# Two products of v in one accumulator bank, and three element-wise steps and one inverse step held behind read-outs, in a hybrid attention/recurrence block

## The chip, the cores and the metric

The kernel runs on one core of a Trainium2 chip, in one launch. The metric is the device time of that core in microseconds (us), the median of several runs. TensorE (PE in the profile) multiplies matrices into accumulator banks, VectorE (DVE), ScalarE (ACT) and GpSimd (POOL) do the element-wise work, and SyncE (SP) issues most DMAs. [...]

## The reference, cut to what matters

One block over 1024 tokens of width 1024: a modulated norm, an input projection, an attention with 8 heads beside a recurrence with 8 heads, a gated merge, and a feed-forward part. The change lies in the attention's v columns and in the recurrence:

```
proj = u @ w_in                       # q, k, v, f | r, k, v, xw, xa, xg | gates
q, k, v, f = split(p_fox)             # v: 1024 x 512, 8 heads of 64
...
kk = k * k_k;  kk = kk / norm(kk)     # recurrence, per head
k_mod = k * (1 + (a - 1) * k_a)
b_vec = kk * a;  a_vec = -kk
def step(state, inp):
    sa = state @ a_t
    state = state * w_t + outer(sa, b_t) + outer(v_t, k_t)
    return state, state @ r_t
```

## The kernel before

All large products are made in a split form: an operand is kept as a high part `hi` and a remainder `lo`, both in TensorE's reduced fp32 type, and a product is `hi*hi + hi*lo + lo*hi`.

The recurrence is done in chunks of 64 tokens. Its eight units are pairs `(p, hf)`: four pairs of heads and two halves of the sequence. A name such as `E2_1` or `kr3_0` carries p and hf at its end. `pre` prepares a unit: decays by a scan (`cum`, `el`, `en`), the scaled keys `bk`, `ar`, products within a chunk (`E`), and the inverse of a unit triangular matrix, 31 steps of two DVE instructions on `E32` and `t32` with the matrix in `M32`, which goes through DRAM and back (`sm`, `M32`, then `se`, `TT`). `main` then runs the chain of states: `xi`, `zi`, `uw`, `mz`, and the eight steps `sp`, after which the output is normalised (`mu`, `va`).

TensorE's instruction order is written out: the class `Weave` keeps a planned clock and puts background products between the recurrence's small ones, one matmul at a time. The background is, in order, the projections for r, k, v of the next units (`ps_rkv`), q and k of the attention (`qk_steps`), then v of the attention (`v_steps`), then the gates (`gate_steps`). The order on DVE, ACT, POOL and SP in this part is chosen by a scheduler when the kernel is built; `add_manual_dep` with `NOSYNC` tells it that one instruction must stand behind another on the same engine, and costs no semaphore.

`v_steps(w, j)` makes half j of v (256 columns) for eight groups t of 128 tokens. A product is 24 matmuls of 128x256, in the first half of an accumulator tile `ps` from `big`, which has two banks that take turns. Its read-out is an ACT copy of the high part into `vs` and a DVE subtraction of the remainder, then a DMA to `d_v`. Product t of half j is called `v{j}_{t}`, its read-out `vs{j}_{t}`.

`shifted` and `qk_steps` are the other users of `big`; their last DVE step reads a bank out (`k`, `r`, `v` of a unit in the one, `ql` in the other). The steps in `pre` that the change touches are these:

```
ts(al, al, V("k_a", p), oka[:, p : p + 1], op0=ALU.mult, op1=ALU.add)
tt(al, al, kk, op=ALU.mult)
tt(bk[:, :, 1, :], c3(al), c3(en), op=ALU.mult)
...
nc.vector.tensor_copy(QA[:, :, 0, :], c3(q))
```

Of the kernel before, what the change touches and what calls it, by code (L numbers as in the profile page):

```python
# [12 lines left out]
ALU = mybir.AluOpType  # L13
# [5 lines left out]
NH = 512  # L19
# [115 lines left out]
def hybrid_block(ctx: ExitStack, tc: tile.TileContext, a, out):  # L135
    nc = tc.nc
    weave = Weave()
    ctx.enter_context(tc.manual_schedule(engines={mybir.EngineType.PE}))

    def mm(o, lhsT, rhs, start, stop, more=False):  # L140

        weave.mm_cost(o, lhsT, rhs)
        nc.tensor.matmul(o, lhsT, rhs, start=start, stop=stop, skip_group_check=more)  # L143
# [5 lines left out]
    def f32(ap):  # L149
        return ap.bitcast(F32)  # L150
# [17 lines left out]
    def V(name, i=0, n=1):  # L168
        o, _ = VEC[name]
        return vec[:, o + i : o + i + n]  # L170
# [78 lines left out]

    marks = {}  # L250
    held = []

    def behind(i, x):
        if x in marks:
# [91 lines left out]
    u = (u_hi, u_lo)  # L346
# [27 lines left out]
    with ExitStack() as es:  # L374
# [4 lines left out]
        def big(name):  # L379
            return pb.tile([128, NH], F32, tag="big", name=name)  # L380
# [4 lines left out]
        def shifted(w, ti, hf, dst, prev, name, by_kt=False):  # L385

            ps = big(f"ps_{name}{hf}")
            yield from gemm_steps(ps, w, u, slice(hf * NH, hf * NH + NH), by_kt=by_kt)
            sh = shp.tile([128, NH + 1], F32, tag="sh", name=f"sh_{name}{hf}")
            if hf == 0:  # L390
                nc.vector.memset(sh[:, 0:1], 0.0)
            else:
                nc.vector.tensor_copy(sh[:, 0:1], prev)
            nc.scalar.activation(sh[:, 1 : NH + 1], ps, AF.Copy, scale=V("mu", ti))
            if hf == 0:
                nc.gpsimd.tensor_copy(prev, sh[:, NH : NH + 1])
            marks["bank"] = stt(dst, ps, omu[:, ti : ti + 1], sh[:, 0:NH], op0=ALU.mult, op1=ALU.add)

        rkv, got, last_col = {}, {}, {}

# [13 lines left out]
        def qk_steps(w, i):  # L414
            sc_ = 0.125 if i < 4 else 1.0
            for hf in range(2):
                cs = slice(hf * NH, hf * NH + NH)
                ps = big(f"qk{i}_{hf}")
                yield from gemm_steps(ps, w, u, cs)
                hi = gsp.tile([128, NH], F32R, tag="sp0", name=f"qh{i}_{hf}")  # L420
                nc.scalar.activation(hi, ps, AF.Copy, scale=sc_)
                lo = gsp.tile([128, NH], F32R, tag="sp0", name=f"ql{i}_{hf}")
                stt(lo, ps, sc_, f32(hi), op0=ALU.mult, op1=ALU.subtract)
                h0 = 2 * (i % 4)
                for t, k, r0 in ((hi, 0, 0), (lo, 0, 64), (hi, 2, 0)) if i < 4 else ((hi, 1, 0), (hi, 1, 64), (lo, 3, 0)):
                    for h in range(2):
                        nc.sync.dma_start(f32(d_st[h0 + h, k, r0 : r0 + 64, cs]), f32(t[h * 64 : h * 64 + 64, :]))
# [274 lines left out]
        def c3(ap):  # L702
            return ap.rearrange("p (c s) -> p c s", s=CH)
# [23 lines left out]
        def pre(k, p, hf):  # L727
# [41 lines left out]
            tt(bk[:, :, 0, :], c3(kr), c3(en), op=ALU.mult)  # L769
            nc.gpsimd.tensor_copy(bk[64:128, :, 2, :], bk[64:128, :, 0, :])  # L770
            tt(ar[:, 1], c3(rr), el[:, :, 1:], op=ALU.mult)
            ts(al, al, V("k_a", p), oka[:, p : p + 1], op0=ALU.mult, op1=ALU.add)
            tt(al, al, kk, op=ALU.mult)
            tt(bk[:, :, 1, :], c3(al), c3(en), op=ALU.mult)
            pcd = chunk_tile("pcd", 3, NCU)
            nc.gpsimd.tensor_copy(pcd, el[:, :, CH])
            rkb = tmp("ksq")
# [33 lines left out]
            for s in range(31):  # L811
                J, W = s // 4 + 1, 31 - s
                tv = t32[:, 0 : J * W].rearrange("p (j w) -> p j w", w=W)
                tt(tv, E32[:, 0:J, s : s + 1].to_broadcast([128, J, W]),  # L814
                   M32[:, s : s + 1, s + 1 : 32].to_broadcast([128, J, W]), op=ALU.mult)
                tt(E32[:, 0:J, s + 1 : 32], E32[:, 0:J, s + 1 : 32], tv, op=ALU.add)  # L816
            se = scr.tile([2, NCU, 2, 32, 32], F32, tag="se", name=f"se{n}")
            for g in range(4):
# [31 lines left out]
            for c in range(NCU):  # L850
                for h in range(2):
                    mm(q[HS[h], c * CH : c * CH + CH], E[HS[1 - h], c, h, 0, :], UV[HS[1 - h], c, h, :], start=True, stop=True)
            nc.vector.tensor_copy(QA[:, :, 0, :], c3(q))
            bp = gen(f"bs{n}")
            yield from head_sums(bp, rkb, tmp("kr", dt=F32R), tmp("al", dt=F32R), True)
            bon = tmp("bon", bufs=2)
# [113 lines left out]
        def v_steps(w, j):  # L970

            for t in range(8):
                ts_ = slice(t * 128, t * 128 + 128)
                ps = big(f"v{j}_{t}")
                n = 0
                for wi, xi in ((0, 0), (0, 1), (1, 0)):
                    for kt in range(KT):
                        c0 = (kt % 4) * 256
                        mm(ps[:, 0:256], u[xi][:, kt, ts_], w[kt // 4][wi][:, c0 : c0 + 256], start=n == 0, stop=n == 23)
                        n += 1  # L980
                        yield
                vs = gsp.tile([128, 4, 2, 64], F32R, tag="sp0", name=f"vs{j}_{t}")
                pv = ps[:, 0:256].rearrange("p (h d) -> p h d", d=64)
                nc.scalar.copy(vs[:, :, 0, :], pv)
                tt(vs[:, :, 1, :], pv, f32(vs[:, :, 0, :]), op=ALU.subtract)
                nc.sync.dma_start(f32(d_v[4 * j : 4 * j + 4, :, t, :]).rearrange("h p x -> p h x"), f32(vs).rearrange("p h a d -> p h (a d)"))
# [730 lines left out]
    ps = wo_do(3, 3)  # L1717
# [380 lines left out]
```

## Time and profile before

| | |
|---|---|
| median of 3 runs | 1640.1 us (1639.86 to 1641.15) |
| profiled execution, its own time | 1639.56 us |
| its span | 1637.8 us |
| mean granted TensorE clock | 0.996 |
| PE busy | 1600.6 us, 98% |
| DVE busy | 1214.5 us, 74% |
| ACT busy | 827.8 us, 51% |
| POOL busy | 157.4 us, 10% |

The v products lie between 319 and 447 us from the span's start; the recurrence with its background ends near 613 us, the attention near 815 us, and the rest is the merge and the feed-forward part. In rows of the timeline the first number is the start in us, the second the length of the row; "x8" means eight instructions of one kind that follow each other; a bracket at the end gives the idle time of the engine before the row and what ended it.

### The profile page before, as it was taken

To read this page: it belongs to the slowest core of one execution; us is meant where nothing else is said; L and a number is where in the kernel's file an instruction comes from. 1 tells how busy PE (TensorE), PEld (TensorE's weight loads), DVE (VectorE), ACT (ScalarE), POOL (GpSimd) and SP (SyncE) were. 2 spreads that over 40 slices of the span, in tenths; PEclk is the share of its full clock that TensorE was granted. 3 is DMA by queue.
4 is the path that set the end of the run, shared out by engine and by line. 5 is a ranking of instruction groups with operands and counts; after the bars stand their busy time and mean duration, and the time that the engine had idled before them with its cause. 6 is when DMAs were issued, how large, how long until landed. Compare 5 with 4: busy or idle time off the path is not lost.

```text
span 1637.8 us, 25963 instructions
## 1 busy us (share of the span) xinstructions
PE 1600.6 (98%) x9678; PEld 1334.4 (81%) x9678; DVE 1214.5 (74%) x2343; ACT 827.8 (51%) x1557; POOL 157.4 (10%) x189
## 2 busy tenths in 40 slices
PE   8999999999999999999999999999999999999998
PEld 7777787888978788888878888888888888888886
DVE  5786787878876536888679548987777777886677
ACT  5563344444455656778623225644444444555455
POOL 0011101111111011333122000000000000000000
PEclk9999999999999999999999999999999999999999
DMA  9496645543333336434197521232332332675363
GB/s 341 128 328 204 177 130 143 141 114 92 115 104 96 97 121 165 128 103 121 44 357 264 187 81 39 71 135 97 114 105 97 101 105 96 232 249 161 122 212 109
DMA packets 123542, 238.79 MB, mean 146 GB/s; under 512 B 42188, under 2 KB 51284, under 8 KB 123416
## 3 DMA queue, kind: packets, MB, share of 16 engines
q1 hardware_dynamic: 114936, 218.77, 41.2%
q0 software_dynamic: 8480, 18.37, 4.2%
q8 instruction: 76, 1.25, 0.3%
q14 instruction: 50, 0.41, 0.1%
HBM read 172.57 MB, written 64.50 MB: 145 GB/s over the span
## 4 chain that ended last, share of the span: by engine, by line
PE 71%; DVE 6%; ACT 2%; issue 1%; DMA 1%; SPq 1%; POOL 0%; DVEq 0%; POOLq 0%; ACTq 0%
PE X L143 15%; PE D L143 13%; PE Y L143 7%; PE gt L143 6%; PE wo L143 5%; PE br L143 4%; PE rk_ps L143 4%; PE W L143 4%; PE ps_rkv L143 3%; PE ov L143 2%; PE lg L143 2%; PE tp L147 1%; PE v L143 1%; PE sp L143 1%; DVE quads L1082 1%
## 5 line engine op out<-in xcount | busy, mean ns | idle before, releaser
L143 PE MATMUL D<-op,op 128*128 128x512 f32 x924 | 209.8, 389 | 0.0
L143 PEld LDWEIGHTS D<-op,op 128*128 128x128 f32 x924 | 173.3, 188 | 36.3 <-DVE op L1302 0.3
L143 PE MATMUL X<-T_m,S 128*128 128x512 f32 x440 | 107.1, 390 | 0.0
L143 PEld LDWEIGHTS X<-T_m,S 128*128 128x128 f32 x440 | 82.4, 188 | 17.8 <-ACT T_m L1781 0.5
L1301 ACT CAST op<-g 128x512 fp32r<-128x512 f32 x77 | 47.8, 621 | 73.0 <-PE D L143 48.2
L1302 DVE TENSOR_TENSOR op<-g,op 128x512 fp32r<-128x512 f32 x77 | 53.0, 689 | 40.8 <-ACT op L1301 40.8
L1560 DVE SCALAR_TENSOR_TENSOR c<-ab,vec,c 128x512 f32<-128x512 f32 x88 | 65.8, 750 | 18.4 <-ACT c L1563 16.8
L814 DVE TENSOR_TENSOR t<-E,M 128x60 f32<-128x60 f32 (+24 forms) x248 | 56.4, 227 | 27.5 <-DMA M<-sm 21.5
L1526 DVE TENSOR_TENSOR A<-ur,A 128x512 fp32r<-128x512 f32 x64 | 44.0, 689 | 38.3 <-ACT A L1522 38.2
L1526 DVE TENSOR_TENSOR S<-ur,S 128x512 fp32r<-128x512 f32 x66 | 45.5, 691 | 35.2 <-ACT S L1522 35.1
L1522 ACT CAST S<-ur 128x512 fp32r<-128x512 f32 x66 | 41.0, 622 | 57.3 <-DVE ur L1515 30.3
L298 DVE TENSOR_TENSOR lo_in<-raw_in,hi_in 128x512 fp32r<-128x512 f32 x84 | 57.6, 726 | 15.8 <-PE gt L143 4.8
L143 PE MATMUL Y<-T_h,A 128*128 128x512 f32 x264 | 63.4, 389 | 0.0
L143 PE MATMUL Y<-T_h,S 128*128 128x512 f32 x264 | 63.3, 389 | 0.0
L1122 DVE TENSOR_TENSOR tl<-tp,th 128x512 fp32r<-128x512 f32 (+1 forms) x80 | 50.0, 631 | 15.3 <-ACT th L1119 14.9
L1522 ACT CAST A<-ur 128x512 fp32r<-128x512 f32 x64 | 39.6, 621 | 42.9 <-PE X L143 33.4
L296 ACT CAST hi_in<-raw_in 128x1024 fp32r<-128x1024 f32 x42 | 43.8, 1048 | 34.2 <-PE qk L143 14.0
L816 DVE TENSOR_TENSOR E<-E,t 128x60 f32<-128x60 f32 (+24 forms) x248 | 56.0, 226 | 6.3
L143 PE MATMUL W<-B_f,A 128*128 128x512 f32 x252 | 60.6, 389 | 0.0
L143 PE MATMUL X<-B_b,A 128*128 128x512 f32 x252 | 60.5, 389 | 0.0
L143 PEld LDWEIGHTS Y<-T_h,S 128*128 128x128 f32 x264 | 49.6, 188 | 10.3
L143 PEld LDWEIGHTS Y<-T_h,A 128*128 128x128 f32 x264 | 49.5, 188 | 10.3
(491 smaller groups left out, 4143.1 us busy)
## 6 DMA issues: line engine op xcount, KB each, us to landing
raw_in<-in_w_in SPq DMA_DIRECT2D x50, 512.0 KB
wm<-in_w_mod SPq DMA_DIRECT2D x48, 512.0 KB
ur<-in_w_up SPq DMA_DIRECT2D x44, 512.0 KB
g<-d_g SPq DMA_DIRECT2D x35, 512.0 KB
d_g<-gs SPq DMA_DIRECT2D x44, 256.0 KB
d_g<-c SPq DMA_DIRECT2D x33, 256.0 KB
d_st<-qh SPq DMA_DIRECT2D x64, 128.0 KB
stA<-d_st POOLq DMA_DIRECT2D x8, 1024.0 KB, 7.3
```

The lines of the kernel that those rows point to most:

```text
L143: nc.tensor.matmul(o, lhsT, rhs, start=start, stop=stop, skip_group_check=more)
L147: nc.tensor.transpose(o, i, eye)
L296: nc.scalar.copy(hi, raw)
L298: nc.vector.tensor_tensor(lo[:, c : c + NH], raw[:, c : c + NH], f32(hi[:, c : c + NH]), op=ALU.subtract)
L814: tt(tv, E32[:, 0:J, s : s + 1].to_broadcast([128, J, W]), M32[:, s : s + 1, s + 1 : 32].to_broadcast([128, J, W]), op=ALU.mult)
L816: tt(E32[:, 0:J, s + 1 : 32], E32[:, 0:J, s + 1 : 32], tv, op=ALU.add)
L1122: tt(tl[:, 0:w], tp[:, 0:w], f32(th[:, 0:w]), op=ALU.subtract)
L1301: nc.scalar.copy(hi, src)
L1302: tt(lo, src, f32(hi), op=ALU.subtract)
L1522: nc.scalar.copy(hi, src)
L1526: tt(lo, src, f32(hi), op=ALU.subtract)
L1560: stt(c, ab[:, x + hf * NH : x + hf * NH + NH], V("conv_w", 22 * x + i), c, op0=ALU.mult, op1=ALU.add)
```

## The change

Three edits, none of which adds or removes a step of the computation. First, two consecutive products of `v_steps` share one accumulator tile: product t with t even takes the first 256 columns, t + 1 the second. Second, in `pre` the three DVE steps on `al` and `bk` are kept in a list for 3000 units of the planned clock; the next DVE read-out in `shifted` or `qk_steps` is given to the scheduler as something that they must stand behind. Third, the first of the 31 inverse steps of a unit must stand behind DVE's copy of `q` into `QA`.

```diff
+    soft = []
+
+    def evac_done(i):
+        for x, t in soft:
+            if weave.now - t < 3000:
+                tc.add_manual_dep(x.ins, i.ins.name, NOSYNC)
+        soft.clear()
+        return i
+    first_step = []
+
+    def after_this(i):
+        for x in first_step:
+            tc.add_manual_dep(x.ins, i.ins.name, NOSYNC)
...
-            marks["bank"] = stt(dst, ps, omu[:, ti : ti + 1], sh[:, 0:NH], op0=ALU.mult, op1=ALU.add)
+            marks["bank"] = evac_done(stt(dst, ps, omu[:, ti : ti + 1], sh[:, 0:NH], op0=ALU.mult, op1=ALU.add))
...
-                stt(lo, ps, sc_, f32(hi), op0=ALU.mult, op1=ALU.subtract)
+                evac_done(stt(lo, ps, sc_, f32(hi), op0=ALU.mult, op1=ALU.subtract))
...
-            ts(al, al, V("k_a", p), oka[:, p : p + 1], op0=ALU.mult, op1=ALU.add)
-            tt(al, al, kk, op=ALU.mult)
-            tt(bk[:, :, 1, :], c3(al), c3(en), op=ALU.mult)
+            soft.clear()
+            soft.append((ts(al, al, V("k_a", p), oka[:, p : p + 1], op0=ALU.mult, op1=ALU.add), weave.now))
+            soft.append((tt(al, al, kk, op=ALU.mult), weave.now))
+            soft.append((tt(bk[:, :, 1, :], c3(al), c3(en), op=ALU.mult), weave.now))
...
-                tt(tv, E32[:, 0:J, s : s + 1].to_broadcast([128, J, W]),
-                   M32[:, s : s + 1, s + 1 : 32].to_broadcast([128, J, W]), op=ALU.mult)
+                i = tt(tv, E32[:, 0:J, s : s + 1].to_broadcast([128, J, W]),
+                       M32[:, s : s + 1, s + 1 : 32].to_broadcast([128, J, W]), op=ALU.mult)
+                if k == 0 and s == 0:
+                    first_step.append(i)
...
-            nc.vector.tensor_copy(QA[:, :, 0, :], c3(q))
+            after_this(nc.vector.tensor_copy(QA[:, :, 0, :], c3(q)))
+            first_step.clear()
...
-                ps = big(f"v{j}_{t}")
+                if t % 2 == 0:
+                    pair = big(f"v{j}_{t}")
+                ps = pair[:, t % 2 * 256 : t % 2 * 256 + 256]
...
-                        mm(ps[:, 0:256], u[xi][:, kt, ts_], w[kt // 4][wi][:, c0 : c0 + 256], start=n == 0, stop=n == 23)
+                        mm(ps, u[xi][:, kt, ts_], w[kt // 4][wi][:, c0 : c0 + 256], start=n == 0, stop=n == 23)
...
-                pv = ps[:, 0:256].rearrange("p (h d) -> p h d", d=64)
+                pv = ps.rearrange("p (h d) -> p h d", d=64)
```

TensorE's order stays the same instruction for instruction; what changes there is the tile that a v product writes and what it waits for. On PE, at the products `v0_4` and `v0_5` of the first half, this stands before (a bracket names the engines on whose semaphores the instruction waits; `sp1_0` is the chain of states of unit 1_0):

```order
L143 MATMUL v0_4_3684<-hi_v00_3289,u_hi_107 128x256 [waits DVE_49]
L143 MATMUL v0_4_3684<-hi_v00_3289,u_hi_107 128x256 x3
L143 MATMUL v0_4_3684<-hi_v01_3296,u_hi_107 128x256 x4
L143 MATMUL v0_4_3684<-hi_v00_3289,u_lo_108 128x256 x4
L143 MATMUL v0_4_3684<-hi_v01_3296,u_lo_108 128x256 x4
L143 MATMUL v0_4_3684<-lo_v00_3290,u_hi_107 128x256 x3
L143 MATMUL sp1_0_3605<-S1_00_3693,Mt_1241 128x64 [waits DVE_49,Activation_49]
L143 MATMUL v0_4_3684<-lo_v00_3290,u_hi_107 128x256
L143 MATMUL v0_4_3684<-lo_v01_3297,u_hi_107 128x256 x4
L143 MATMUL v0_5_3718<-hi_v00_3289,u_hi_107 128x256 [waits DVE_49]
L143 MATMUL v0_5_3718<-hi_v00_3289,u_hi_107 128x256 x3
```

The same place on PE now, where the tile of `v0_5` carries the name of `v0_4`:

```order
L143 MATMUL v0_4_3682<-hi_v00_3289,u_hi_107 128x256 [waits PE_49]
L143 MATMUL v0_4_3682<-hi_v00_3289,u_hi_107 128x256 x3
L143 MATMUL v0_4_3682<-hi_v01_3296,u_hi_107 128x256 x4
L143 MATMUL v0_4_3682<-hi_v00_3289,u_lo_108 128x256 x4
L143 MATMUL v0_4_3682<-hi_v01_3296,u_lo_108 128x256 x4
L143 MATMUL v0_4_3682<-lo_v00_3290,u_hi_107 128x256 x3
L143 MATMUL sp1_0_3604<-S1_00_3691,Mt_1241 128x64 [waits DVE_49,Activation_49]
L143 MATMUL v0_4_3682<-lo_v00_3290,u_hi_107 128x256
L143 MATMUL v0_4_3682<-lo_v01_3297,u_hi_107 128x256 x4
L143 MATMUL v0_4_3682<-hi_v00_3289,u_hi_107 128x256 [waits DVE_49]
L143 MATMUL v0_4_3682<-hi_v00_3289,u_hi_107 128x256 x3
```

Nothing moved, but the waits did. Counted through the semaphores, `v0_5` waited before for DVE's remainder step of `vs0_3`, the product that had its bank earlier; now it waits for that of `vs0_4`, the product just ahead of it. `v0_4` waited before for `vs0_2`; now it waits for nothing on DVE. The other pairs are alike.

On DVE, where unit 0_0 is in its inverse and the remainder `ql5_1` of a q/k product is read out (`bon0_0` is a bonus term, `cum0_1` the scan of the next unit, `lo_in17` a weight's remainder), this stands before:

```order
L814 TENSOR_TENSOR t320_0_1513<-E320_0_1511,M320_0_1506 128x50
L816 TENSOR_TENSOR E320_0_1511<-E320_0_1511,t320_0_1513 128x2x25
L814 TENSOR_TENSOR t320_0_1513<-E320_0_1511,M320_0_1506 128x48
L857 TENSOR_TENSOR bon0_0_1688<-bs0_0_1665,v00_636 128x512
L744 SCALAR_TENSOR_TENSOR cum0_1_1694<-cst2_117,cum0_1_1694 128x256 x2
L816 TENSOR_TENSOR E320_0_1511<-E320_0_1511,t320_0_1513 128x2x24
L298 TENSOR_TENSOR lo_in17_1725<-raw_in17_1722,hi_in17_1724 128x512 x2
L423 SCALAR_TENSOR_TENSOR ql5_1_1714<-qk5_1_1622,qh5_1_1712 128x512
```

And now, on DVE at the same place:

```order
L828 TENSOR_TENSOR t320_0_1513<-E320_0_1511,M320_0_1506 128x50
L874 TENSOR_TENSOR bon0_0_1688<-bs0_0_1665,v00_636 128x512
L757 SCALAR_TENSOR_TENSOR cum0_1_1694<-cst2_117,cum0_1_1694 128x256 x2
L832 TENSOR_TENSOR E320_0_1511<-E320_0_1511,t320_0_1513 128x2x25
L311 TENSOR_TENSOR lo_in17_1725<-raw_in17_1722,hi_in17_1724 128x512 x2
L436 SCALAR_TENSOR_TENSOR ql5_1_1714<-qk5_1_1622,qh5_1_1712 128x512
L828 TENSOR_TENSOR t320_0_1513<-E320_0_1511,M320_0_1506 128x48
```

Two inverse steps went from ahead of `ql5_1` to behind it. A few rows earlier, `QA0_0`'s copy of q went from behind the first two inverse steps to ahead of them.

On DVE, around the read-out of `v1_4` (`vs1_4`; `E322_1` and `t322_1` are the inverse of unit 2_1, `ar3_0`, `kr3_0`, `bk3_0`, `al3_0` belong to unit 3_0), this stands before:

```order
L814 TENSOR_TENSOR t322_1_4562<-E322_1_4560,M322_1_4555 128x75
L768 SCALAR_TENSOR_TENSOR kr3_0_4886<-kr3_0_4886,vec_72,al3_0_4808 128x512
L816 TENSOR_TENSOR E322_1_4560<-E322_1_4560,t322_1_4562 128x5x15
L769 TENSOR_TENSOR bk3_0_4888<-kr3_0_4886,en3_0_4815 128x8x64
L772 TENSOR_SCALAR al3_0_4808<-al3_0_4808,vec_72,quads_82 128x512
L814 TENSOR_TENSOR t322_1_4562<-E322_1_4560,M322_1_4555 128x70
L773 TENSOR_TENSOR al3_0_4808<-al3_0_4808,k30_4094 128x512
L816 TENSOR_TENSOR E322_1_4560<-E322_1_4560,t322_1_4562 128x5x14
L985 TENSOR_TENSOR vs1_4_4997<-v1_4_4900,vs1_4_4997 128x4x64
```

And now:

```order
L832 TENSOR_TENSOR E322_1_4556<-E322_1_4556,t322_1_4558 128x7x7
L781 SCALAR_TENSOR_TENSOR kr3_0_4880<-kr3_0_4880,vec_72,al3_0_4803 128x512
L828 TENSOR_TENSOR t322_1_4558<-E322_1_4556,M322_1_4551 128x42
L782 TENSOR_TENSOR bk3_0_4882<-kr3_0_4880,en3_0_4810 128x8x64
L786 TENSOR_SCALAR al3_0_4803<-al3_0_4803,vec_72,quads_82 128x512
L832 TENSOR_TENSOR E322_1_4556<-E322_1_4556,t322_1_4558 128x7x6
L787 TENSOR_TENSOR al3_0_4803<-al3_0_4803,k30_4090 128x512
L828 TENSOR_TENSOR t322_1_4558<-E322_1_4556,M322_1_4551 128x35
L1004 TENSOR_TENSOR vs1_4_4991<-v1_4_4894,vs1_4_4991 128x4x64
```

The inverse is further along when DVE gets here (the steps are those of width 7 in place of 15 and 14), but the long steps of unit 3_0 ahead of `vs1_4` are the same, in the same order.

## The prediction

> **What bounds the kernel now.** The page comes first: the span, and how much of it TensorE is busy.
>
> ```profile
> span 1637.8 us, 25963 instructions
> PE 1600.6 (98%) x9678; PEld 1334.4 (81%) x9678; DVE 1214.5 (74%) x2343; ACT 827.8 (51%) x1557; POOL 157.4 (10%) x189
> ```
>
> PE is idle for 37.2 us of 1637.8. So a wait that is taken from PE is worth at most its own length, and any new wait of PE is paid in full unless a later wait of PE shrinks for it. The busy times by stage (columns: stretch, length, then busy time and count of PE, PEld, DVE, ACT, POOL, then TensorE's granted clock) say where that can be. The stretches are: before the v products, the v products, the rest of the recurrence.
>
> ```profile
> 140.00:319.00 179.00, 174.65 (x1400) 141.96 (x1399) 136.96 (x370) 75.11 (x135) 26.95 (x39) 1.00 0.58 157
> 319.00:452.00 133.00, 131.61 (x1477) 117.20 (x1476) 112.17 (x324) 61.72 (x127) 20.44 (x31) 1.00 0.40 114
> 452.00:613.40 161.40, 158.23 (x1369) 128.97 (x1368) 93.22 (x242) 90.94 (x169) 18.72 (x21) 1.00 0.33 102
> ```
>
> PE's idle time is 4.35, 1.39 and 3.17 us there, 8.9 us in all. That is the most that any better order on DVE in these stages can bring. DVE is not the bound (77, 84 and 58% busy), but it works its queue strictly in order, so a read-out waits for what stands ahead of it.
>
> **The shared bank.** The two banks of `big` took turns: the read-out of product t had all 24 matmuls of product t + 1 to hide behind. Now the second product of each pair begins with a wait for the read-out of the first (the order on PE shows a wait for DVE there, and its count is the remainder step of the product just ahead). PE has nothing else queued ahead of it, apart from one pair. So what each pair costs can be read from before: from the moment when PE went on to the second product, to the end of DVE's step of the first. PE restarts 0.06 us after such a step: the step that began at 437.78 below ended at 438.20, and PE restarted at 438.26. The rows, in order of time, of `v0_0`/`v0_1`, `v0_2`/`v0_3` and so on to `v1_6`/`v1_7`:
>
> ```profile
> 323.03 0.77 PE L143 MATMUL v<-hi_v,u_hi 128*128 128x256 f32 x5
> 324.46 0.42 DVE L985 TENSOR_TENSOR vs<-v,vs 128x256 fp32r<-128x256 f32 x1
> ...
> 332.23 1.96 PE L143 MATMUL mz<-E,Wt 64*64 64x128 f32 x32
> 332.94 0.42 DVE L985 TENSOR_TENSOR vs<-v,vs 128x256 fp32r<-128x256 f32 x1
> 336.14 1.22 PE L143 MATMUL v<-hi_v,u_hi 128*128 128x256 f32 x8
> ...
> 342.85 0.98 PE L143 MATMUL v<-hi_v,u_hi 128*128 128x256 f32 x6 [0.47 <-DVE vs L985]
> 343.79 0.42 DVE L985 TENSOR_TENSOR vs<-v,vs 128x256 fp32r<-128x256 f32 x1
> ...
> 351.09 0.88 PE L143 MATMUL v<-hi_v,u_hi 128*128 128x256 f32 x6
> 351.70 0.42 DVE L985 TENSOR_TENSOR vs<-v,vs 128x256 fp32r<-128x256 f32 x1
> ...
> 411.83 1.11 PE L143 MATMUL v<-hi_v,u_hi 128*128 128x256 f32 x8
> 413.62 0.42 DVE L985 TENSOR_TENSOR vs<-v,vs 128x256 fp32r<-128x256 f32 x1
> ...
> 421.83 0.40 PE L143 MATMUL v<-hi_v,u_hi 128*128 128x256 f32 x2
> 424.00 0.42 DVE L985 TENSOR_TENSOR vs<-v,vs 128x256 fp32r<-128x256 f32 x1
> ...
> 434.20 1.12 PE L143 MATMUL v<-hi_v,u_hi 128*128 128x256 f32 x8
> 437.78 0.42 DVE L985 TENSOR_TENSOR vs<-v,vs 128x256 fp32r<-128x256 f32 x1
> 438.26 1.22 PE L143 MATMUL v<-hi_v,u_hi 128*128 128x256 f32 x8 [0.78 <-DVE vs L985]
> ...
> 441.68 0.88 PE L143 MATMUL v<-hi_v,u_hi 128*128 128x256 f32 x6
> 442.05 0.37 ACT L984 CAST vs<-v 128x256 fp32r<-128x256 f32 x1 [0.51 <-DMA d_v<-vs]
> 442.76 0.42 DVE L985 TENSOR_TENSOR vs<-v,vs 128x256 fp32r<-128x256 f32 x1
> ```
>
> Pair 1: 324.88 + 0.06 - 323.03 = 1.91 us. Pair 2: nothing, since `mz`, `sp` and `yp` lie between its products (332.23 to 336.14) and the read-out is done at 333.36. Pair 3: PE was free at 342.85 - 0.47 = 342.38, so 344.21 + 0.06 - 342.38 = 1.89. Pair 4: 1.09. Pair 5: 414.04 + 0.06 - 411.83 = 2.27. Pair 6: 424.42 + 0.06 - 421.83 = 2.65. Pair 7: 438.26 - 434.20 = 4.06, because DVE is in the long steps of unit 3_0, and these still stand ahead of `vs1_4`. Pair 8: 443.18 + 0.06 - 441.68 = 1.56; its 0.51 us for the DMA of an older `vs` should go, since PE's shift gives that DMA more time: 1.05. Sum: 14.92 us.
>
> Two waits go: the first product of a pair now needs a bank that was read out long before, so the brackets of 0.47 and 0.78 us vanish, 1.25 us. Net 13.67 us.
>
> What is queued behind the waiting matmul on PE: the rest of the product, and with it `zi`, `uw`, `va`, `p` and the chain of states, so the recurrence itself is late by as much. DVE's inverse steps don't wait for PE and run ahead meanwhile, which keeps DVE free later; the order shows that, with width 7 in place of 15 ahead of `vs1_4`. I take the waits as read from before, though their DVE steps may fall a little differently. The shortest that any can be is pair 4's path, 1.09 us (ACT copy, DVE step and the handovers): seven times that, 7.6 us, is the lower end. The upper end is 15.43, with pair 8 unmended.
>
> [...]
>
> **The three steps, and the first inverse step.** What they can bring is the waits of PE for DVE's read-outs ahead of the v products. There are two, and these rows show them with what stands ahead.
>
> ```profile
> 180.11 0.68 DVE L853 COPY QA<-q 128x512 f32<-128x512 f32 x1
> ...
> 183.29 0.21 DVE L816 TENSOR_TENSOR E<-E,t 128x50 f32<-128x50 f32 x1
> ...
> 186.74 0.69 DVE L423 SCALAR_TENSOR_TENSOR ql<-qk,qh 128x512 fp32r<-128x512 f32 x1
> 187.48 2.12 PE L143 MATMUL qk<-u_hi,hi_in 128*128 128x512 f32 x8 [2.26 <-DVE ql L423]
> ...
> 245.48 0.54 DVE L772 TENSOR_SCALAR al<-al,vec,quads 128x512 f32<-128x512 f32 x1
> ...
> 247.39 0.73 PE L143 MATMUL ps_rkv<-u_hi,hi_in 128*128 128x512 f32 x2 [1.36 <-DVE k L397]
> ```
>
> The copy into `QA` moves ahead of the first inverse step, into time when DVE waits for `M32`: about 0.5 to 0.6 of its 0.68 us is won. Two inverse steps, each like the one at 183.29 at some 0.24 us from start to start, go behind `ql`: 0.5. So `ql` comes about 1.0 us earlier and PE's 2.26 shrinks to 1.26. At 247.39 the first of the three steps now stands behind the read-out of `k`: 0.54 us and a handover, but PE is also there 1.0 us sooner, and DVE, which started that inverse about as much sooner, keeps pace: I take 0.65. Together 1.65, between 0 (if DVE is only late elsewhere) and 3.62 (both waits gone). The price of the edits is a later `bk`, by one read-out step, 0.69 us as `ql`'s above, if the products `p` that need it follow at once; PE shows no wait for `bk` in this stage before (the two bracketed rows are its only waits for DVE there), so other products lie between and I take nothing.
>
> **What is given back.** After the v products PE waits here; the DVE rows show why.
>
> ```profile
> 458.40 0.43 DVE L872 STREAM_TRANSPOSE X<-TT 32x256 f32<-32x256 f32 x1 [3.23 <-DMA TT<-se]
> 458.86 0.69 DVE L953 SCALAR_TENSOR_TENSOR y<-mu,y 128x512 f32<-128x512 f32 x1
> ...
> 461.88 0.49 PE L143 MATMUL va<-Zts,blk_r 128*128 128x512 f32 x1 [0.61 <-ACT Zts L719]
> 463.24 0.50 PE L143 MATMUL va<-Wts,blk_r 128*128 128x512 f32 x1 [0.86 <-POOL Wts L722]
> ```
>
> The transposes of unit 2_1 wait for `TT`, which comes from an inverse that DVE makes without PE; behind them stands `y`, and behind that `va`. With PE some 13 us late, `TT` is there first, and 0.61 + 0.86 = 1.47 us go. The other waits of this stage hang on PE's own results and move with it.
>
> **The sum**, against the profiled execution's own 1639.56 us (its span and 1.8 us around it): 1639.56 + 13.67 - 1.65 - 1.47 = 1650.1. The median is 0.5 above that execution, so 1650.5 us is the forecast, 0.6% slower than 1640.1. Its chance is 0.80.
>
> **Rivals.** First, the waits are short: DVE, which has run ahead, is free at each read-out, so that all seven cost 1.09. For it speaks the further inverse; against it the long steps ahead of `vs1_4`, which didn't move. 1639.56 + 7.6 - 1.25 - 1.65 - 1.47 = 1642.8. Chance 0.08.
>
> Second, the other side: the pair does not serialise, as the two halves are different words of the bank. Then only the 1.25 and the 1.65 us are left, 1636.7. It decides at the first matmul of the second product: if DVE's count there were already reached, PE would go straight on. Against it stands the count, which is that of the product just ahead. Chance 0.02.
>
> Third, a long wait costs the clock as well. Early in the kernel, after a wait and matmuls of one column, TensorE ran at half its rate:
>
> ```profile
> 42.73 3.09 PE L143 MATMUL mps<-cst,acc 128*128 128x1 f32 x16 [1.83 <-DVE acc L482]
> ...
> 44.00:46.00 2.00, 2.00 (x10) 2.00 (x11) 0.30 (x3) 0.00 (x0) 0.00 (x0) 0.50 0.00 0
> ...
> 48.00:50.00 2.00, 2.00 (x6) 1.61 (x6) 2.00 (x5) 1.20 (x2) 0.00 (x0) 0.50 0.00 0
> ```
>
> From 44 to 50 us the clock is 0.50, which loses 3 us. The wait of 2.26 us at 187.48 did no such thing (clock 1.00 in its stage), but pair 7 would idle for 4.06. If it trips there: 1650.5 + 3.0 = 1653.5, and twice would be 1656.5. Chance 0.10. [...]
>
> **How the numbers follow.** A measurement of this kernel can tell 0.2%, 3.3 us, from no change. The forecast's own bounds (the waits between 7.6 and 15.43, the gains between 0 and 3.62) go from about 1643 to 1654; in its middle I allow 5 us either way, and reach to the third rival: 1645.5 to 1655.5. Slower by over 0.2% means above 1643.4: all of the forecast and of the third rival, and half of the first, 0.94. Within 0.2%: the rest of the first, 0.04. Faster: the second, 0.02.
>
> **What would show it.** Right: PE waits for `vs` in seven places between 319 and 465, 12 to 16 us in all, the longest at `v1_5`; the stretch from the first v product to the first gate grows by 13 to 15 us; the waits at `va` gone; PE's wait for `ql` about 1.3. Wrong: fewer than five such waits, or their sum under 8 us, or the granted clock under 0.98 in that stretch.

## The result, and the profile after

The changed kernel takes 1656.2 us (median of 4 runs, 1654.36 to 1657.18), the kernel before 1640.0 on the same chip (1638.53 to 1641.15): a ratio of 1.0096, interval 1.0084 to 1.0109. The forecast was 1650.5 with 1645.5 to 1655.5. Slower was right, and so were the waits that make up most of it; the size is 5.7 us short and the range ends 0.7 us too low.

The profiled execution took 1654.36 us, 14.8 more than that of before, and its span is longer by the same 14.8. The head of the page, and two rows of the chain of waits on PE between 100 and 640 us (columns: total wait, how often, the longest):

```profile
span 1652.6 us, 25953 instructions
PE 1603.9 (97%) x9678; PEld 1337.9 (81%) x9678; DVE 1214.7 (74%) x2343; ACT 827.4 (50%) x1557; POOL 157.0 (10%) x189
...
PE v L143 <- DVE vs L1004: 15.8, 7, 4.7
PE ps_rkv L143 <- DVE k L410: 0.6, 1, 0.6
```

DVE, ACT and POOL do what they did. PE is busy for 3.3 us more and idle for 11.5 us more: the new waits are idle time, but PE's own work has become slower as well. The wait for `ql`, 2.26 us before, is below what this view lists.

The seven waits in the timeline of PE (start, length, what, idle time before and what ended it), in the order of the pairs 1, 3, 4, 5, 6, 7, 8, and the two `va` products behind them:

```profile
320.87 0.86 PE L143 MATMUL v<-hi_v,u_hi 128*128 128x256 f32 x5 [1.75 <-DVE vs L1004]
...
343.74 0.98 PE L143 MATMUL v<-hi_v,u_hi 128*128 128x256 f32 x6 [1.90 <-DVE vs L1004]
...
353.12 0.98 PE L143 MATMUL v<-hi_v,u_hi 128*128 128x256 f32 x6 [0.96 <-DVE vs L1004]
...
416.24 1.21 PE L143 MATMUL v<-hi_v,u_hi 128*128 128x256 f32 x8 [2.10 <-DVE vs L1004]
...
431.22 0.55 PE L143 MATMUL v<-hi_v,u_hi 128*128 128x256 f32 x2 [4.72 <-DVE vs L1004]
...
448.90 2.07 PE L143 MATMUL v<-hi_v,u_hi 128*128 128x256 f32 x8 [3.43 <-DVE vs L1004]
...
457.90 0.98 PE L143 MATMUL v<-hi_v,u_hi 128*128 128x256 f32 x6 [0.96 <-DVE vs L1004]
...
477.44 0.40 PE L143 MATMUL va<-Zts,blk_r 128*128 128x512 f32 x1
477.67 0.39 PE L143 MATMUL va<-Wts,blk_r 128*128 128x512 f32 x1
```

They add up to 15.82 us. The row at 448.90 shows the second effect: eight matmuls take 2.07 us, where eight of the same kind took 1.11 to 1.22 before. The granted clock says why. In this execution it is 0.50 in five stretches: from 42.41 us for 6.83, from 322.30, 431.53 and 448.59 for 3.41 each, and from 1650.1 to the end, where PE has nothing left to do. From start to start these lie 82, 32, 5 and 352 times 3.41 us apart, so on one grid of such windows through the whole execution. Here are windows of that grid (columns: limits, length, PE busy and its instructions, TensorE's granted clock, DMA share, GB/s):

```profile
318.89:322.30 3.41, 1.66 (x40) 1.00 0.69 198
322.30:325.71 3.41, 3.41 (x18) 0.50 0.38 126
...
414.46:417.87 3.41, 1.63 (x12) 1.00 0.69 208
417.87:421.28 3.41, 3.41 (x89) 1.00 0.45 106
...
428.11:431.53 3.42, 0.31 (x2) 1.00 0.54 149
431.53:434.94 3.41, 3.41 (x32) 0.50 0.48 154
445.18:448.59 3.41, 0.29 (x3) 1.00 0.00 0
448.59:452.00 3.41, 3.10 (x14) 0.50 0.26 77
```

After each of three windows in which PE was idle for about half or more (busy for 1.66, 0.31 and 0.29 us), the next window has half the clock. By estimate, a window of 3.41 us at half the clock does 1.7 us less work: three are 5.1 us. The window at 414.46 was busy for 1.63 us, idle for as large a part as the first, and the clock behind it stayed at 1.00 (PE's busy time is modelled). What a halved window costs can be followed on PE, whose order is the same in both traces: it restarts 2.16 us earlier than before behind the first pair's wait (320.87 against 323.03), but reaches the next product that follows `mz`, `sp` and `yp` only 0.54 us earlier (335.60 against 336.14), with no wait between. That is 1.6 us lost. Before, the clock was 1.00 in all three stretches from 140 to 613 us.

### The profile page after: what moved, and what is told of

It is laid out like the page before. It is cut to its first block, busy times and chain, and to the rows that moved or that the text cites. A ratio compares the mean times of both kernels' runs of the same rounds, so it can differ in the third digit from the quotient of the medians.

```text
span 1652.6 us, 25953 instructions
## 1 busy us (share of the span) xinstructions
PE 1603.9 (97%) x9678; PEld 1337.9 (81%) x9678; DVE 1214.7 (74%) x2343; ACT 827.4 (50%) x1557; POOL 157.0 (10%) x189
## 3 DMA queue, kind: packets, MB, share of 16 engines
q8 instruction: 76, 1.25, 0.3%
## 4 chain that ended last, share of the span: by engine, by line
PE 84%; DVE 7%; ACT 3%; DMA 3%; issue 2%; SPq 0%; POOL 0%; DVEq 0%; ACTq 0%
PE X L143 15%; PE D L143 13%; PE Y L143 7%; PE ps_rkv L143 6%; PE qk L143 5%; PE gt L143 5%; PE wo L143 5%; PE br L143 4%; PE W L143 4%; PE rk_ps L143 3%; PE ov L143 2%; PE v L143 2%; PE lg L143 2%; PE tp L147 1%; PE p L143 1%
```

## The experiments

Each was compared with the kernel before on the same chip. "Both edits" means the three steps and the first inverse step.

**The shared bank alone, and the two edits alone.** The first has the new `v_steps` in the kernel before, the second the old `v_steps` in the changed kernel:

```
 e1: + pair = big(...) for even t, ps = half of pair   (nothing else of the change)
 e2: - pair = big(...)   + ps = big(f"v{j}_{t}")       (both edits stay)
```

> The kernel before with the shared bank alone; the three steps and the first inverse step stand as before. Theory (the waits for the read-out just ahead and the clock that falls after the long ones make the loss, and the two edits to DVE's order give about 3 us back): seven waits for vs, 13 to 16 us in all, and 1658 to 1660 us. Rival (the edits to the order lengthen the waits, and pair 6 waited 4.72 us because of them): waits near the 14.9 us read from before, pair 6 at 2.7, and 1653 us or less.

> The changed kernel with one bank for each product of v, as before. Theory: the waits of 2.26 us for ql and of 1.36 us for k shrink by about 3.0 us and nothing else moves: 1636.5 to 1637.5 us. Rival (the edits to the order cost something of their own): 1640 us or more.

The bank alone: 1657.36 us, ratio 1.0113 (1.0097 to 1.0129), just under the first theory's band. The edits alone: 1637.91, ratio 0.9989 (0.9980 to 0.9998), 0.4 us above its theory's band and 2.1 below its rival's. The product of the two ratios is 1.0102; the whole change has 1.0096. So the sharing is the loss and the edits are a small gain, barely clear of no change. From the waits on PE of the first, then of the second:

```profile
PE v L143 <- DVE vs L987: 14.0, 7, 3.4
PE qk L143 <- DVE ql L423: 1.6, 1, 1.6
PE ps_rkv L143 <- DVE k L397: 1.4, 1, 1.4
```

```profile
PE v L143 <- DVE vs L1002: 1.7, 2, 1.2
...
PE qk L143 <- DVE ql L436: 0.6, 1, 0.6
PE ps_rkv L143 <- DVE k L410: 0.6, 1, 0.6
```

In the first, the waits add up to 14.0 us and the sixth pair waits 2.88, about as its rival had it; but the time is far above the rival's, and four windows behind the waits are halved, one of them behind the fifth pair. The changed kernel shows the same short sixth wait in another execution (the last experiment below), so the edits are not what makes it long.

**Sharing without the wait for the product just ahead.** Products 0 and 2 of each four share one bank, 1 and 3 the other:

```
-  if t % 2 == 0: pair = big(f"v{j}_{t}")
-  ps = pair[:, t % 2 * 256 : t % 2 * 256 + 256]
+  if t % 4 < 2: two[t % 2] = big(f"v{j}_{t}")
+  ps = two[t % 2][:, t // 2 % 2 * 256 : t // 2 % 2 * 256 + 256]
```

> The changed kernel, two products still share a bank, but they alternate: products 0 and 2 in one bank, 1 and 3 in the other, so that each wait is for the product before the last. Theory (it is the wait for the product just ahead, not the sharing): no wait for vs over 0.8 us, granted clock 1.00 between 319 and 452 us, 1635.5 to 1637.5 us. Rival (sharing a bank costs by itself, as the matmuls and the read-outs of one bank slow each other): 1645 us or more, with v's matmuls or read-outs longer than before.

1637.75 us, ratio 0.9991 (0.9982 to 1.0000): as fast as one bank for every product, 0.25 us above the theory's band and far below the rival's. PE waits twice for a read-out, 1.5 us in all, the longer 1.1 (I had said 0.8 at most). Two products in a bank cost nothing that can be told here (0.9991 against 0.9989) as long as another product lies between the one and the other; what costs is the wait for the read-out just ahead. One window of this execution is halved all the same, behind waits that the kernel before has too (0.7 and 0.9 us at `va` here):

```profile
459.32:462.73 3.41, 1.84 (x8) 1.00 0.56 160
462.73:466.15 3.42, 3.42 (x39) 0.50 0.19 70
```

**What the clock costs: the waits filled with idle matmuls.** Ahead of five second products PE gets 128x512 matmuls into the next pair's bank; their results are overwritten. They keep PE busy while the read-out is made.

```
+ elif (j, t) in FILL:                # {(0,1): 6, (0,5): 7, (1,1): 8, (1,3): 19, (1,5): 13}
+     ahead.append(big(f"v{j}_{t + 1}"))
+     for _ in range(FILL[j, t]): nc.tensor.matmul(ahead[0], ...)
```

> The changed kernel, where PE does 6, 7, 8, 19 and 13 idle matmuls of 128x512 (0.227 us each, 12.0 us in all, into the next pair's bank, overwritten later) ahead of the second products of pairs 1, 3, 5, 6 and 7, in the time in which it only waited. Theory (part of the loss is the clock, which halves when PE waits): clock 1.00 in the v products, the waits for vs fall to 3 to 5 us, and the time falls by 4 to 6 us to 1650 to 1652. Rival (the clock's fall falls into the waits and costs nothing; what is beyond the forecast comes from longer waits): 1655 to 1658 us.

1654.98 us, ratio 1.0097 (1.0082 to 1.0111): by the time alone the rival is right, at its lower end. The trace says something else. No window between 60 and 550 us is halved, the first `va` behind the v products comes 3.2 us earlier than in the changed kernel (474.23 against 477.44), and then PE loses it again at 549 us. Its rows of the fill, that `va`, and the late wait; between them the DVE row, from the same trace, on which that wait hangs:

```profile
426.07 4.60 PE L999 MATMUL v<-hi_v,u_hi 128*128 128x512 f32 x19
...
474.23 0.40 PE L143 MATMUL va<-Zts,blk_r 128*128 128x512 f32 x1
...
536.45 0.19 DVE L828 TENSOR_TENSOR t<-E,M 128x31 f32<-128x31 f32 x1 [3.37 <-DMA M<-sm]
...
549.36 0.43 PE L143 MATMUL sp<-S,Mt 128*128 128x64 f32 x2 [2.51 <-ACT S L950]
```

In the changed kernel DVE's wait for the same `M` is 1.81 us (at 538.75) and PE's for the same `S` 0.93 us (at 551.65). The late `M` makes DVE late, so a gate's DVE step is late, ACT waits 4.33 us for that step, and `S` stands behind it on ACT; the window that this empties costs one at half the clock as well (three 128x512 matmuls from 550.39 take 1.00 us, where three from 552.67 take 0.85 in the changed kernel). `M` is read back 4.90 us after the DMAs that write `sm` begin to be issued (527.30, 532.20), where the changed kernel takes 3.25 (531.17, 534.42): the read waits 2.3 us for the write to land, in place of 0.6. Why the write took longer is open; the build also orders some other instructions anew around the fill.

**The fill at three pairs only**, those behind which the clock had fallen: `FILL = {(0, 1): 6, (1, 3): 19, (1, 5): 13}`.

> The changed kernel with idle 128x512 matmuls (6, 19 and 13 of them, their results overwritten) only ahead of the second products of the first, sixth and seventh pair, where TensorE's clock was halved behind the wait. Theory: PE reaches the steps behind the v products 3.4 to 5 us earlier than in the changed kernel, though it has as much to do or wait for; 1651 to 1653 us, unless the wait of 2.5 us for the state S at 549 us, which the kernel with five fills had, comes again (then 1654 to 1655.5). Rival (the halved windows cost nothing): PE is there less than 1 us earlier, 1655.5 to 1657 us.

1656.66 us, ratio 1.0103 (1.0089 to 1.0116). The time lies in the rival's band, and PE reaches `va` no earlier than in the changed kernel (478.30 against 477.44), but this doesn't decide between the two: the wait for `S` came again (2.38 us), and now the clock fell behind the third and the fifth pair, which have no fill. One of the four executions took 1653.04 us, with a mean clock of 0.997 where the others have 0.994 and 0.995. The rows of the two pairs:

```profile
343.77 1.61 PE L143 MATMUL v<-hi_v,u_hi 128*128 128x256 f32 x6 [2.18 <-DVE vs L1011]
...
418.84 2.01 PE L143 MATMUL v<-hi_v,u_hi 128*128 128x256 f32 x8 [2.10 <-DVE vs L1011]
```

```profile
340.43:343.85 3.42, 1.24 (x11) 1.00 0.20 61
343.85:347.26 3.41, 3.41 (x16) 0.50 0.46 117
415.53:418.94 3.41, 1.31 (x12) 1.00 0.67 177
418.94:422.35 3.41, 3.41 (x14) 0.50 0.43 130
```

Put beside the changed kernel this is the cleanest pair of rows of the study. The fifth pair's wait is 2.10 us in both; there PE was busy for 1.63 us of the window, the clock stayed at 1.00, and the eight matmuls behind it took 1.21 us; here the wait lies within one window, PE was busy for 1.31 us of it, the clock fell to 0.50, and they take 2.01. Of these two waits of one length, one cost clock and the other didn't, by where the grid lay.

**The long waits and the short ones apart.** Sharing for the sixth and seventh pair only, and for the other six only:

```
- if t % 2 == 0:
+ if t % 2 == 0 or 4 * j + t // 2 + 1 not in (6, 7):     # the other: (1, 2, 3, 4, 5, 8)
```

> The changed kernel, but of the eight pairs only the sixth and the seventh (v1_2/v1_3 and v1_4/v1_5) share a bank; every other product has one of its own. One bank for every product measured 1637.9 us. Theory (the waits are paid, and TensorE's clock is then halved for one window of 3.41 us behind each wait that fills more than about half of such a window, 1.7 us lost each time): waits of 2.6 to 4.7 and 3.4 to 4.1 us, 6.7 to 8.1 in all, less the 1.2 us that PE waited for v1_4's read-out before, and two windows, 3.4 us: 1646.8 to 1648.3 us, and the clock record shows two windows at 0.50 between 420 and 455 us. Rival (only the waits are paid, the clock is an accident of the records): 1643.4 to 1644.9 us.

> The other six pairs share a bank (the first to the fifth and the eighth), the products of the sixth and seventh have one each. Waits of 1.75, 0, 1.90, 0.96, 2.10 and 0.96 us, 7.7 in all, less about 0.5 us that PE waited for a read-out before: 1645.1 us if only the waits are paid (the rival, within 1 us). Theory: a wait of 0.96 us can't empty half of a window of 3.41 us and costs no clock, one of 1.75 to 2.10 us does so only where it lies within one window, so none to three windows at 0.50, each behind one of those three waits and each 1.7 us: 1645 to 1650 us, differing from execution to execution by steps of about 1.7 us. In the trace each halved window follows a window in which PE was busy for less than about 0.55 of the time.

The long ones: 1643.29 us, ratio 1.0024 (1.0015 to 1.0034), 0.1 us below the rival's band and 3.5 below the theory's; but the windows that the theory wanted are there:

```profile
419.64:423.05 3.41, 0.55 (x4) 1.00 0.54 163
423.05:426.46 3.41, 3.41 (x32) 0.50 0.50 154
436.70:440.12 3.42, 0.66 (x6) 1.00 0.00 0
440.12:443.53 3.41, 3.41 (x18) 0.50 0.26 77
```

My sum for it was wrong in other places. PE's waits for `vs` are 6.1 us in all, 4.4 more than with the edits alone, and the 1.45 us of waits at `va` go, which I had left out. With two windows: 1637.0 (the edits' 0.9989 of this chip's 1639.0) + 4.4 + 3.4 - 1.45 = 1643.4. Without the windows it would be 1640.0.

The short ones: 1649.75, ratio 1.0066 (1.0053 to 1.0078), at the upper end of the theory and above the rival. PE's waits for `vs` are 10.0 us in all, not 7.7: the eighth pair's first product, which takes over the bank of `v1_4`, waits 1.84 us for that read-out, and its second 1.43 in place of 0.96. And two windows in a row are halved, behind the first pair's wait of 1.73 us; PE was busy all through the window ahead of the second, which the theory doesn't allow:

```profile
446.41 1.22 PE L143 MATMUL v<-hi_v,u_hi 128*128 128x256 f32 x8 [1.84 <-DVE vs L1004]
451.42 0.98 PE L143 MATMUL v<-hi_v,u_hi 128*128 128x256 f32 x6 [1.43 <-DVE vs L1004]
...
318.42:321.84 3.42, 1.69 (x14) 1.00 0.50 147
321.84:325.25 3.41, 3.41 (x43) 0.50 0.49 165
325.25:328.66 3.41, 3.41 (x17) 0.50 0.22 77
```

Waits of 0.96 us never cost clock in any of the traces: in the changed kernel it is 1.00 from 349.60 to 364.00 us and from 452.00 to 465.00, around those at 353.12 and 457.90.

**The two edits apart**, with one bank for every product; the first without the edit of the first inverse step, the second without `soft`:

```
 e7: - if k == 0 and s == 0: first_step.append(i)
 e8: - soft.append((ts(al, al, ...), weave.now)) ...   + ts(al, al, ...) ...
```

> One bank for every product, and only the edit of the three steps; the first inverse step stays where it was. Theory: the three steps are what shortened PE's wait for the read-out of k (1.36 us in the kernel before, 0.6 with both edits), and the wait for ql is the other edit's: k about 0.6, ql still 2 us or more, time 1638.5 to 1639.5 us. Rival (the edits act together, ql comes sooner because DVE has less ahead of it): ql below 1.2 us and the time within 0.5 us of the 1637.9 of both edits.

> One bank for every product, and only the edit of the first inverse step; the three steps stand where they stood. Theory: PE's wait for ql falls from 2.26 to about 0.6 us, that for k stays at 1.3 to 1.6 us; time 1638 to 1639 us. Rival: the wait for ql stays above 1.2 us and the time at 1639 to 1640 us.

The three steps alone: 1637.98, ratio 0.9994 (0.9985 to 1.0003); PE waits 1.3 us for `ql` and 0.3 for `k`. The first inverse step alone: 1639.35, ratio 0.9998 (0.9989 to 1.0006); 0.5 for `ql` and 1.5 for `k`. So the `k` wait is the three steps', as I had it. The `ql` wait differs between executions: it is 2.26 and 1.65 us in two kernels with neither edit, and from nothing to 1.0 us in those with both. So 0.5 with the first inverse step alone is a clear fall (I had sized both edits together at 1.0), and 1.3 with the three steps alone is not shown to be one. Neither run fits one theory in all: the first ends inside the rival's 0.5 us with `ql` just above the rival's 1.2, and the second has the theory's waits and the rival's time. Apart, neither edit can be told from no change.

**Looking for a faster version.** One bank for every product, both edits, and v's read-outs ahead of the three steps too; then the same with the alternating banks:

```
- tt(vs[:, :, 1, :], pv, f32(vs[:, :, 0, :]), op=ALU.subtract)
+ evac_done(tt(vs[:, :, 1, :], pv, f32(vs[:, :, 0, :]), op=ALU.subtract))
```

> One bank for every product, both order edits, and the read-outs of the v products also go ahead of the three steps where these are next. In the kernel with both order edits PE still waits twice for such a read-out, 1.7 us in all (1.21 us at v1_5, whose step stands behind two of the three). Theory: the longer wait falls by about 1 us, the kernel ends 0.5 to 1 us earlier than with the order edits alone, 0.9983 to 0.9987 of the kernel before. Rival: the steps that now stand behind make the next read-out, or bk's users, late by as much: no wait is shorter in sum, 0.9987 to 0.9995.

> Banks shared by every other product (the first and third, the second and fourth), so that a product waits for the read-out of the one before last, with both order edits and the read-outs of the v products ahead of the three steps. Theory: as with one bank for every product, since the read-outs have a whole product to hide behind: within 0.0006 of the ratio of that kernel with the same order edits. Rival: the doubled sharing costs at least one wait of over 0.8 us more, 0.9992 or more.

0.9994 (0.9985 to 1.0003) and 0.9989 (0.9980 to 0.9998). In the first PE's waits for `vs` do fall from 1.7 to 1.1 us, but the time doesn't follow: a miss. In its profiled execution the first wait at `va` is 1.2 us in place of 0.6, and the window behind it is halved. The second behaves as its theory has it. Three versions end about 0.1% faster than before: the edits alone, with alternating banks, and this one. They can't be told from each other.

**The changed kernel once more.**

> The changed kernel, unchanged, on another execution. Its profiled execution took 1654.36 us with three windows of 3.41 us at half the clock between 310 and 470 us. Theory: the waits are the same within 0.2 us, but where the windows' limits lie against them is chance, so that there are two to five halved windows, behind other waits perhaps, and the profiled execution's time is 1654.4 us plus 1.7 for each window more than three, less 1.7 for each fewer, within 1 us (halved windows in the first 60 us counted alike). Rival: the number of windows differs and the time doesn't follow, or the waits themselves differ by more than 0.5 us.

1655.89 us (two runs, ratio 1.0099, 1.0069 to 1.0128); the profiled execution took 1654.59 us with four halved windows in the v stretch, one more than the other. The theory wanted 1656.1 within 1: a miss, and by its letter the rival holds, for the time and for one wait. The fourth is behind the fifth pair, as in the kernel with three fills, and the sixth pair's wait is 2.96 us instead of 4.72:

```profile
416.88 1.22 PE L143 MATMUL v<-hi_v,u_hi 128*128 128x256 f32 x8 [2.10 <-DVE vs L1004]
...
431.55 0.53 PE L143 MATMUL v<-hi_v,u_hi 128*128 128x256 f32 x2 [2.96 <-DVE vs L1004]
```

```profile
414.83:418.24 3.41, 1.36 (x11) 1.00 0.75 197
418.24:421.66 3.42, 3.42 (x38) 0.50 0.51 128
```

Against the other execution PE restarts 0.64 us later at the fifth pair (416.88, 416.24) and only 0.33 later at the sixth (431.55, 431.22): it came later to a wait that ends at its own time. In the changed kernel DVE waits, ahead of the sixth read-out, for a matrix that goes through DRAM, and then has the queue to work off:

```profile
420.97 0.19 DVE L828 TENSOR_TENSOR t<-E,M 128x31 f32<-128x31 f32 x1 [4.78 <-DMA M<-sm]
...
430.75 0.42 DVE L1004 TENSOR_TENSOR vs<-v,vs 128x256 fp32r<-128x256 f32 x1
```

Here the same row begins at 421.35, with 4.52 us for the same DMA. So the 1.7 us, by estimate, of the window behind the fifth pair are hidden by the sixth pair's wait: here a halved window cost nothing, because a late wait followed it.

## Why the prediction was wrong, and what it had right

By its own steps, on the profiled execution:

| term | forecast | measured |
|---|---|---|
| seven waits at the pairs | 14.92 | 15.82 |
| waits that vanish (0.47 + 0.78) | -1.25 | -1.25 |
| `ql` (2.26 gone) and `k` (1.36 to 0.6) | -1.65 | -3.0 |
| waits at `va` given back | -1.47 | -1.47 |
| clock | 0 | up to 5.1 |
| sum | 10.55 | 15.2 |
| own time | +10.5 (1650.1) | +14.8 (1654.36) |

The measured terms overshoot by 0.4 us. Two amounts outside them make that up: PE was 0.87 us ahead already at a q/k product before any of these waits (178.25 against 179.12), and behind the recurrence it loses 0.46 us more (14.34 us later than before at 492.70 against 478.36, 14.8 at the end).

The median lies 1.8 us above this execution, and the forecast allowed 0.5; the other executions have no trace. Their mean clock is on record: 0.993, 0.992 and 0.991, against 0.994 here. One window of 3.41 us at half the clock takes 0.001 off a mean over 1653 us, so by an estimate from these figures they had about one to three such windows more. That is enough for the 1.8 us, though the order of the times doesn't follow that of the clocks.

**Right.** Slower, and by waits of PE: it waits in seven places, once for each pair but the second, whose products `mz`, `sp` and `yp` still cover the read-out. The sum is 6% off. The three short pairs (1, 3, 5) are within 0.2 us of their rows of before, since their path is only what stands between matmul and read-out. The waits at `va` went. The bank alone and the edits alone moved the time to the two sides that the terms said. The rivals "all waits short" and "the pair does not serialise" are out: the waits are twice 7.6 us.

**The step that failed: the clock.** The sum put it at nothing, and three halved windows cost up to 5.1 us of the 14.8. The prediction had it as its third rival, with a chance of 0.10, for the seventh pair alone. It named a clock under 0.98 in the stretch as what would make the forecast wrong, and the clock is 0.96:

```profile
319.00:452.00 133.00, 118.00 (x1274) 104.02 (x1273) 102.96 (x302) 52.48 (x107) 18.16 (x28) 0.96 0.34 98
```

The reason for so low a chance was the wait of 2.26 us before, which had left the clock at 1.00, so that only the one wait of 4.06 seemed long enough. That row was read without its grid. On the grid of before that wait is cut in two:

```profile
183.17:186.59 3.42, 2.05 (x9) 1.00 0.56 128
186.59:190.00 3.41, 2.52 (x11) 1.00 0.45 88
```

Neither window is idle for half of its length. A wait of 1.75 us inside one window (320.87 in the changed kernel) was followed by a clock of 0.50, one of 2.26 across two was not. The windows don't lie alike against the work in each execution: in two of the changed kernel they begin at 414.46 and at 414.83. Windows with PE busy for 1.66 and 1.69 of 3.41 us were followed by half the clock. From this the working, an estimate after the fact, should have been: a wait of 3.43 us or more empties half of some window of 3.41, and one of 1.75 to 2.10 us in about half of the executions (such waits of the pairs 1, 3 and 5 did in 8 of 14 cases of the five traces that have them); three or four windows, 5 to 7 us, less what a later wait hides. That is 1654 to 1657.

**Smaller misses.** The longest wait is the sixth pair's (4.72 us, forecast 2.65), not the seventh's (3.43, forecast 4.06). I took the DVE rows of before as they stood, and allowed only that they "may fall a little differently". Here is DVE's wait for `M` ahead of the sixth read-out, in the kernel before and in the one that shares only the sixth and seventh pair:

```profile
417.54 0.39 DVE L814 TENSOR_TENSOR t<-E,M 128x31 f32<-128x31 f32 x1 [1.72 <-DMA M<-sm]
...
416.02 0.19 DVE L828 TENSOR_TENSOR t<-E,M 128x31 f32<-128x31 f32 x1 [2.32 <-DMA M<-sm]
```

`M` comes 3.43 us later in the changed kernel (420.97), which is less than PE's own delay there (it begins this wait at 426.50, against 421.83 before: 4.67). The read-out begins 6.75 us later (430.75 against 424.00), because DVE needs 9.78 us from `M` to it in place of 6.46: seven more instructions of the inverse and a step on `y` stand ahead of it in the order that the build chose, and one inverse step takes 1.24 us in place of 0.18. In the kernel that shares only the sixth and seventh, DVE has the order of before at this place, needs 6.24 us (to 422.26), and the wait is 2.87. So what makes this wait long is the work now ahead of the read-out on DVE, and not the late DMA.

The forecast also said that the stretch from the first v product to the first gate would grow by 13 to 15 us. It grew by 20.4, from 127.15 us (319.36 to 446.51) to 147.54 (315.29 to 462.83). The forecast's own terms give 13.67 for it; of the 6.7 us beyond that the clock's 5.1 and the waits' 0.9 are 6.0. The order edits brought about 1.4 us more than I gave them in this execution, which hid a part of the error. And the bounds "from about 1643 to 1654" are not what their terms give: with all of them at the low end the median is 1641.3, at the high end 1652.8. The range was not built on them alone, so that changes little.

Not tried: the second product of a pair without its wait for the read-out, since reading and writing would then be unordered.

## What to carry to other kernels

Here two results shared a bank at no cost that can be told (a ratio of 0.9991, against 0.9989 with a bank for each) where another product stood between them; where they followed each other, PE paid the whole path of the read-out, 0.96 to 4.72 us at seven of eight pairs, and that path is read from the trace of before. Price a new wait of TensorE by where its idle time falls on the clock's windows, not by its length alone: in these traces one that left PE busy for more than 0.54 of a window of 3.41 us cost only itself, and one that left it busy for 0.47 or less was each time followed by a window at half the clock, by estimate 1.7 us more. And a wait read from the old trace holds only while nothing ahead of it moves: compare the new order on the engine that is waited for, up to each read-out, before the old rows are used.

## What the hardware showed

Between 100 and 640 us of all fourteen traces, TensorE's clock fell to 0.50 for windows of 3.41 us, each but one behind a window in which PE was busy for 0.54 of the time or less. Every window there with a busy share up to 0.47 was followed by a halved one (14 of 14), and of those with 0.48 to 0.54 five were and six were not. Above that there is one case only: behind a single wait of 1.73 us two windows in a row were halved (321.84 and 325.25 in the run of the short pairs), and the first of these, in which PE was busy throughout (3.41 of 3.41 us), stands ahead of the second.

The mean clock goes with the time in kernels without the change too. On the chip on which the search for a faster version ran, the five executions of the kernel before with a mean clock of 0.998 took 1636.25 to 1637.80 us, and the five with 0.994 or 0.995 took 1638.08 to 1640.76.

Idle matmuls into a bank that is free, 6 to 19 of 128x512 ahead of five products, kept the clock at 1.00 from 310 to 490 us, but here the 3.2 us that they won were lost again 75 us later.
